# A hybrid decoder step: the 32x32 inverses of the delta net on one compact tile, and the last feed-forward block in halves of 320 and 256 tokens

## The chip, the cores and the metric

The kernel runs on one core of one Trainium2 chip. The metric is the device time of one execution in microseconds (us): the median of several timed runs. One further execution is recorded by the hardware profiler, and all traces here are of such an execution. A core has TensorE (PE, matmuls; its weight loads are a row of their own, PEld), VectorE (DVE), ScalarE (ACT), GpSimd (POOL) and SyncE (SP), which here issues the DMAs.

## The reference

Two decoder layers are computed in fp32 for 512 prompt tokens and 8 x 8 sample tokens, 576 in all, with a model width of 1024. Layer 0 mixes by trailing means (pooling), layer 1 by a gated delta rule over 16 value heads in chunks; each mixer is followed by a feed-forward network (SwiGLU, inner width 2816). Norms stand before and after each.

```
x = x + rms_norm(m, norm_mix_post[i])
h = rms_norm(x, norm_ffn_pre[i])
x = x + rms_norm(swiglu(h, ffn_w_in[i], ffn_w_out[i]), norm_ffn_post[i])
```

The delta rule needs, for each chunk and head, the solution of a unit lower triangular system:

```
t_mat = a_mat + jnp.eye(CHUNK, dtype=jnp.float32)
u = solve(t_mat, v * beta[..., None])
w = solve(t_mat, kb * jnp.exp(gc)[..., None])
```

The outputs are the 576 rows of y and the new states.

## The kernel before, in words

**Tiling.** Activations lie with channels on the partitions and tokens along the free axis. Every fp32 matrix is split into a high and a low part; `mm3` (line 979) makes one product from three matmuls for each tile of 128 channels. Weights come in tiles by a DMA (`wraw`), ACT makes the high part (`wh`) and DVE or POOL the low one (`wl`). Tokens are worked on in two ranges: `HALVES` (256 and 320) where prompt and sample are told apart, and `EVEN` (288 and 288, line 31) in the output part of the feed-forward.

**Order.** Nothing is issued as it is written. Class `Plan` records every operation with an estimated cost, makes a list schedule over the five engines, and refines it (`refined`, line 533; `moved`, line 552) by shifts of the priorities that are drawn from the seeds in the table `CHOSEN` (line 79); each string of the table is one pass over the whole program. `EITHER` operations go to DVE or POOL, as the plan finds room. Where the plan leaves TensorE idle, it inserts matmuls of a constant into a bank that is free (`ps_w`, line 527); they compute nothing that is used.

**PSUM.** `bank(tag)` (line 904) hands out the eight banks in rings: A is banks 0 to 2, B is 3 to 5, n0 and n1 are 6 and 7, and the mixer has rings of its own over the same banks (`m`, for the projections, is banks 3 and 4).

**Delta net.** The 16 heads are worked on in four groups. In `core` (line 1903) each group builds a tile `Uw` of 128 partitions by 16 systems (four heads, four spans of 128 tokens) by 128 columns. `inv32` (line 1407) inverts the four 32x32 blocks on the diagonal of all 16 systems at once. Four DVE transposes, one for each block of 32 partitions, read the block out of `Uw` with a stride of 128 elements and write it, each element twice, to `A` (in the trace `ia`); 31 steps of two DVE operations each work on `X` (in the trace `ii`); four DVE transposes put the result back into `Uw`. The blocks of 64 and 128 are then made from these by matmuls. `inv32` is woven with the sample tokens' work, and the planner lays projections of the next group beside it.

**Last feed-forward.** `ffn` (line 1148) computes the inner channels in blocks of 5, 5, 5 and 7 tiles, and adds each block's output product into `y`. In the last block (from line 1219) the two halves follow one another: for each of eight output tiles `m`, `out` (line 1173) makes the product of half 0 in ring A or of half 1 in ring B, DVE adds it to `y` (in the trace `yo`), ACT squares it (`nsq`), the squares are summed (`nacc`), and `turn_y` (line 2165) scales it (`nh`) and transposes it on TensorE, in pieces of at most 128 tokens (`PIECES`, line 34: three pieces a half), so that tokens lie on the partitions. Half 0 is transposed into ring B, half 1 into ring A. After four tiles ACT copies the transposed pieces to SBUF (`yT`); the last four stay in PSUM. `finish1` (line 2182) then sums the squares over the channels (TensorE into `ps_n`), takes square root (ACT) and reciprocal (DVE) into `nrc`, and for each piece DVE multiplies and adds the residual (`xa`, `xb`), reading `yT` and the PSUM banks; SP sends the rows out. The residual is transposed beforehand by `turn_x` (line 2146), before the gate part of this feed-forward, written to DRAM (`x_t`) and fetched again by `back_x` (line 2157).

Of the kernel before, what the change touches and what calls it, by code (L numbers as in the profile page):

```python
# [11 lines left out]
F32 = mybir.dt.float32  # L12
# [8 lines left out]
P = 128  # L21
D = 1024
# [11 lines left out]
PIECES = (((0, 128), (128, 128), (256, 32)), ((288, 128), (416, 96), (512, 64)))  # L34
# [22 lines left out]
class Plan:  # L57
# [755 lines left out]
def hybrid_kernel(  # L813
# [334 lines left out]
    def ffn(layer, x, y, wts, xp, ap_, tp, head, finish, beside=None, turn=None):  # L1148
# [24 lines left out]
        def out(bi, f0, m, hf, w):  # L1173
            s = state[hf.i]
            at = slice(hf.o, hf.o + hf.n)
            ps = bank("AB"[hf.i])[:, :hf.n]
            mm3(ps, w, lambda k: tuple(v[:, at] for v in acts[f0 + k]), blocks[bi])
            yc = y[:, m, at]
            if bi == 0:
# [1055 lines left out]
```

## Time and profile before

| | |
|---|---|
| three timed runs, median (lowest to highest) | 1526.5 us (1526.38 to 1527.4) |
| the profiled execution | 1525.06 us |
| its span, first to last instruction | 1523.3 us |
| mean granted TensorE clock | 0.997 |
| HBM read, written | 165.60 MB, 30.52 MB |

A line of a group gives operation, tile written <- tiles read, shapes and count, then busy us, mean ns of one, and the idle time of the engine before it with what ended it. A line of the table of stages gives a stretch in us from the start of the span, its length, the busy time (and instructions) of each engine, the granted TensorE clock, the DMA engines' busy share and GB/s. A line of the timeline gives start, duration, engine, line and operation; equal neighbours are merged. Operations all carry the line of the planner that issues them (L531), so tiles tell them apart.

### The profile page before, as it was taken

Reading aid. Unit: us, or ns where it says so; the run is one execution under the profiler, and the core shown is the slowest. Engines: PE = TensorE matmul, PEld = TensorE weight load, DVE = VectorE, ACT = ScalarE, POOL = GpSimd, SP = SyncE. Lnnn points to the kernel's source line nnn. Section 1 sums busy time; section 2 is a strip of 40 time slices with the busy share of each in tenths; the row PEclk is TensorE's granted clock in tenths of the full one; section 3 lists DMA queues with packets and bytes.
Section 4 is the critical chain, followed back from the end, with each engine's and each line's share of the span. In section 5 each row is a group of like instructions: output and inputs, shape, how many; then the busy total and the mean of one; then the engine's idle time right before and its main releaser. Section 6 shows DMA issues by size and latency. Waiting matters only on the chain.

```text
span 1523.3 us, 30379 instructions
## 1 busy us (share of the span) xinstructions
PE 1501.0 (99%) x11850; PEld 1452.8 (95%) x11850; DVE 1155.7 (76%) x2284; ACT 840.6 (55%) x1815; POOL 129.4 (8%) x269
## 2 busy tenths in 40 slices
PE   8999999999999999999999999999999999999997
PEld 7999999999999899899899899999999999999997
DVE  6993566678688698997899799667896476766865
ACT  7753543435466975764763764545565453534553
POOL 4210000000011010121120120100110000000000
PEclk9999999999999999999999999999999999999999
DMA  6563323233457433335433544657765333233263
GB/s 190 156 188 110 98 74 111 67 99 104 148 170 204 114 88 111 102 103 147 111 112 93 147 127 128 202 158 220 240 184 155 109 87 96 83 89 110 66 196 99
DMA packets 344902, 197.86 MB, mean 130 GB/s; under 512 B 13547, under 2 KB 337740, under 8 KB 344751
## 3 DMA queue, kind: packets, MB, share of 16 engines
q1 hardware_dynamic: 344759, 195.92, 44.6%
q8 instruction: 93, 1.52, 0.4%
q14 instruction: 50, 0.41, 0.1%
HBM read 165.60 MB, written 30.52 MB: 129 GB/s over the span
## 4 chain that ended last, share of the span: by engine, by line
PE 88%; DVE 6%; ACT 3%; DMA 2%; issue 1%; POOL 0%; SPq 0%; DVEq 0%; ACTq 0%; POOLq 0%
PE ps_B L531 29%; PE ps_A L531 26%; PE ps_m L531 19%; PE ps_s L531 5%; PE ps_k L531 5%; PE ps_x L531 2%; PE ps_e L531 1%; DVE wl L531 1%; PE ps_n L531 1%; DVE Uw L531 1%; DMA vt<-z_d 1%; DVE ac L531 1%; ACT wh L531 1%; DMA wraw<-in_gdn_w_in_dram 0%; DMA yo<-y_d 0%
## 5 line engine op out<-in xcount | busy, mean ns | idle before, releaser
L531 ACT ACTIVATE wh<-wraw 128x1024 fp32r<-128x1024 f32 (+4 forms) x239 | 232.5, 978 | 201.5 <-PE ps_B L531 79.6
L531 DVE TENSOR_TENSOR wl<-wraw,wh 128x1024 fp32r<-128x1024 f32 (+4 forms) x231 | 258.3, 1122 | 76.0 <-ACT wh L531 40.3
L531 PE MATMUL ps_m<-hH,wh 128*128 128x320 f32 (+1 forms) x832 | 251.5, 313 | 0.0
L531 PE MATMUL ps_m<-hL,wh 128*128 128x320 f32 (+1 forms) x832 | 247.5, 306 | 0.1
L531 PE MATMUL ps_m<-hH,wl 128*128 128x256 f32 (+1 forms) x832 | 245.8, 308 | 0.1
L531 PEld LDWEIGHTS ps_m<-hH,wh 128*128 128x128 f32 x832 | 155.1, 190 | 4.0 <-issue 1.0
L531 PEld LDWEIGHTS ps_m<-hL,wh 128*128 128x128 f32 x832 | 156.0, 190 | 2.0 <-issue 0.8
L531 PEld LDWEIGHTS ps_m<-hH,wl 128*128 128x128 f32 x832 | 154.7, 190 | 1.7 <-issue 0.4
L531 PE MATMUL ps_B<-hH,wh 128*128 128x320 f32 (+1 forms) x444 | 127.8, 304 | 0.2
L531 PE MATMUL ps_B<-hL,wh 128*128 128x320 f32 (+1 forms) x444 | 127.1, 304 | 0.0
L531 PE MATMUL ps_B<-hH,wl 128*128 128x320 f32 (+1 forms) x444 | 127.1, 304 | 0.0
L531 PE MATMUL ps_A<-hH,wh 128*128 128x256 f32 (+1 forms) x432 | 119.4, 292 | 0.0
L531 PE MATMUL ps_A<-hL,wh 128*128 128x256 f32 (+1 forms) x432 | 117.7, 290 | 0.0
L531 PE MATMUL ps_A<-hH,wl 128*128 128x256 f32 (+1 forms) x432 | 117.5, 291 | 0.1
L531 PE MATMUL ps_B<-aL,wh 128*128 128x288 f32 x352 | 100.0, 296 | 0.0
L531 PE MATMUL ps_B<-aH,wl 128*128 128x288 f32 x352 | 99.2, 297 | 0.7 <-DVE wl L531 0.7
L531 PE MATMUL ps_B<-aH,wh 128*128 128x288 f32 x352 | 99.1, 298 | 0.5 <-DVE xa L531 0.5
L531 PE MATMUL ps_A<-aL,wh 128*128 128x288 f32 x352 | 98.3, 296 | 0.0
L531 PE MATMUL ps_A<-aH,wl 128*128 128x288 f32 x352 | 97.7, 297 | 0.0
L531 PE MATMUL ps_A<-aH,wh 128*128 128x288 f32 x352 | 97.1, 297 | 0.0
L531 PEld LDWEIGHTS ps_B<-hH,wh 128*128 128x128 f32 x444 | 81.7, 188 | 0.7 <-ACT wh L531 0.6
L531 DVE SCALAR_TENSOR_TENSOR ac<-u,cwt,ac 128x600 f32<-128x600 f32 x96 | 79.5, 837 | 3.3 <-ACT ac L531 3.1
(463 smaller groups left out, 4040.8 us busy)
## 6 DMA issues: line engine op xcount, KB each, us to landing
wraw<-in_ffn_w_in_dram SPq DMA_DIRECT2D x77, 512.0 KB
wraw<-in_gdn_w_in_dram SPq DMA_DIRECT2D x56, 512.0 KB
graw<-in_ffn_w_in_dram SPq DMA_DIRECT2D x33, 512.0 KB
wraw<-in_ffn_w_out_dram SPq DMA_DIRECT2D x32, 448.0 KB
wraw<-in_gdn_w_out_dram SPq DMA_DIRECT2D x24, 512.0 KB
wraw<-in_ffn_w_out_dram SPq DMA_DIRECT2D x32, 320.0 KB
St<-in_state_gdn_rec_dram SPq DMA_DIRECT2D x32, 256.0 KB
out_dram<-St SPq DMA_DIRECT2D x32, 256.0 KB
```

The source lines that it names most:

```text
L531: calls[e](*a, **k)
```

## The change

In the delta net, `inv32` first copies the four diagonal blocks with ACT into one compact tile of 128 partitions by 32 by 16 (the second half of `XT`, which is free then). One DVE transpose over all 128 partitions makes `A` from it; at the end one DVE transpose over all partitions writes `X` to the compact tile, and four ACT copies put the blocks back into `Uw`.

In the last block of the last feed-forward the halves are 320 and 256 tokens (`LAST`). Both halves' products go to ring A, both halves' transposes to ring B. The pieces are 128, 128, 64 and 128, 128; the last piece holds the last 64 prompt and all 64 sample tokens and is sent out by two DMAs. In a half without a short piece, the square root and reciprocal of that piece fall away. The residual is transposed in the same five pieces. The seeds of the planner's table are others: four passes with 2281 seeds in place of six with 3239.

```diff
-PIECES = (((0, 128), (128, 128), (256, 32)), ((288, 128), (416, 96), (512, 64)))
+LAST = (Half(0, 0, 320), Half(1, 320, 256))
+PIECES = (((0, 128), (128, 128), (256, 64)), ((320, 128), (448, 128)))
...
         def out(bi, f0, m, hf, w):
...
-            ps = bank("AB"[hf.i])[:, :hf.n]
+            ends = turn is not None and bi == len(blocks) - 1
+            ps = bank("A" if ends else "AB"[hf.i])[:, :hf.n]
...
-                for hf in EVEN:
+                for hf in EVEN if turn is None else LAST:
...
+        D32 = XT[:, 1].rearrange("p (i h) -> p i h", h=16)
         for b in range(4):
             s = slice(32 * b, 32 * b + 32)
-            DVE.transpose(A[s], W[s, :, 32 * b:32 * b + 32].rearrange("p h i -> p i h").unsqueeze(2)
-                          .to_broadcast([32, 32, 2, 16]))
-            yield 1.2
+            ACT.activation(D32[s], W[s, :, s].rearrange("p h i -> p i h"), AF.Copy)
+        DVE.transpose(A, D32.unsqueeze(2).to_broadcast([P, 32, 2, 16]))
+        yield 1.2
...
+        DVE.transpose(XT[:, 1].rearrange("p (i j) -> p i j", j=32), X.rearrange("p j i -> p i j"))
         for b in range(4):
             s = slice(32 * b, 32 * b + 32)
-            DVE.transpose(W[s, :, 32 * b:32 * b + 32].rearrange("p h (i d) -> p i d h", d=2),
-                          X[s].rearrange("p j i -> p i j"))
+            ACT.activation(W[s, :, s].rearrange("p h i -> p i h"), D32[s], AF.Copy)
             yield 0.6
...
         def turn_y(hf, c):
...
-                    yT[o, c // 4] = bank("BA"[hf.i], (P, 4, P))[:n].rearrange("p c f -> p (c f)")
+                    yT[o, c // 4] = bank("B", (P, 4, P))[:n].rearrange("p c f -> p (c f)")
...
         def finish1(hf, acc):
...
-            for r, q in ((slice(0, P), slice(0, 2)), (slice(0, last), slice(2, 3))):
-                ACT.activation(rc[r, q], ps[r, q], AF.Sqrt, bias=eps_c[r], scale=1.0 / D)
-                DVE.reciprocal(rc[r, q], rc[r, q])
+            for r, q in ((slice(0, P), slice(0, whole)), (slice(0, hf.n % P), slice(whole, whole + 1))):
+                if r.stop:
+                    ACT.activation(rc[r, q], ps[r, q], AF.Sqrt, bias=eps_c[r], scale=1.0 / D)
+                    DVE.reciprocal(rc[r, q], rc[r, q])
...
-                SP.dma_start(y_prompt[0, o:o + n] if o < SEQ else y_sample.rearrange("b t d -> (b t) d"), xT[o])
+                m = min(n, SEQ - o)
+                SP.dma_start(y_prompt[0, o:o + m], xT[o][:m])
+                if m < n:
+                    SP.dma_start(y_sample.rearrange("b t d -> (b t) d"), xT[o][m:])
```

More of the change, by code (lines that the diff above doesn't have):

```diff
@@ L2148, in turn_x @@
                 for c4 in range(0, NC, 4):
-                    ps = bank("n%d" % (o >= EV), (P, 4, P))[:n]
+                    ps = bank("n%d" % (o >= LAST[1].o), (P, 4, P))[:n]
                     for c in range(4):
@@ L2159, in back_x @@
             xa = xp.tile([P, 4, D], F32, name="xa", tag="x", bufs=1)
-            xb = ap_.tile([P, 2, D], F32, name="xb1", tag="tb", bufs=1)
+            xb = ap_.tile([P, D], F32, name="xb1", tag="tb", bufs=1)
             for i, (o, n) in enumerate(PIECES[0] + PIECES[1]):
-                xT[o] = (xa[:n, i] if i < 4 else xb[:n, i - 4])
+                xT[o] = xa[:n, i] if i < 4 else xb[:n]
                 SP.dma_start(xT[o], x_t[o:o + n])
@@ L2170, in turn_y @@
             if c == 3:
-                sbs = [ap_.tile([P, k, 4 * P], F32, name="yT", tag="graw", bufs=2) for k in (2, 1)]
+                sbs = [ap_.tile([P, 2, 4 * P], F32, name="yT", tag="graw", bufs=2) for _ in PIECES[hf.i][::2]]
             for i, (o, n) in enumerate(PIECES[hf.i]):
                 if c % 4 == 0:
-                    yT[o, c // 4] = bank("BA"[hf.i], (P, 4, P))[:n].rearrange("p c f -> p (c f)")
+                    yT[o, c // 4] = bank("B", (P, 4, P))[:n].rearrange("p c f -> p (c f)")
                 ps = yT[o, c // 4]
@@ L2186, in finish1 @@
             rc = halftile(tp, "nrc", hf, 1, (P, 4))
-            last = PIECES[hf.i][2][1]
+            whole = hf.n // P
             for i, (o, n) in enumerate(PIECES[hf.i]):
-                n = n if i == 2 else P
-                a = acc[0]
-                PE.matmul(ps[:n, i:i + 1], a[:, i * P:i * P + n] if i < 2 else a[:, EV - n:], ones[:, 0:1],
-                          start=True, stop=True)
-            for r, q in ((slice(0, P), slice(0, 2)), (slice(0, last), slice(2, 3))):
-                ACT.activation(rc[r, q], ps[r, q], AF.Sqrt, bias=eps_c[r], scale=1.0 / D)
-                DVE.reciprocal(rc[r, q], rc[r, q])
+                PE.matmul(ps[:n, i:i + 1], acc[0][:, o - hf.o:o - hf.o + n], ones[:, 0:1], start=True, stop=True)
+            for r, q in ((slice(0, P), slice(0, whole)), (slice(0, hf.n % P), slice(whole, whole + 1))):
+                if r.stop:
+                    ACT.activation(rc[r, q], ps[r, q], AF.Sqrt, bias=eps_c[r], scale=1.0 / D)
+                    DVE.reciprocal(rc[r, q], rc[r, q])
             for i, (o, n) in enumerate(PIECES[hf.i]):
```

341 rows, old and new, of the table CHOSEN are left out of this document.

## The prediction

> **What bounds the kernel now.** I read the page's first part, then a table of stages, then the timeline where the table shows a hole.
>
> ```profile
> span 1523.3 us, 30379 instructions
> PE 1501.0 (99%) x11850; PEld 1452.8 (95%) x11850; DVE 1155.7 (76%) x2284; ACT 840.6 (55%) x1815; POOL 129.4 (8%) x269
> ```
>
> TensorE is busy 1501.0 of 1523.3 us, so work taken from another engine is worth only what TensorE waits for that engine. The profiled execution took 1525.06 us, 1.8 more than its span; the median of the three timed runs is 1526.5. Differences are worked out in the trace and put on the median.
>
> ```profile
> core 0: us, PE busy (x) PEld busy (x) DVE busy (x) ACT busy (x) POOL busy (x), PEclk, DMA share, GB/s
> 487.00:1047.00 560.00, 554.71 (x4749) 516.28 (x4748) 469.01 (x1100) 353.91 (x1000) 78.39 (x154) 1.00 0.45 128
> 560.00:925.00 365.00, 361.01 (x3138) 335.45 (x3137) 324.73 (x777) 227.35 (x681) 58.29 (x122) 1.00 0.40 114
> 1180.00:1440.00 260.00, 260.00 (x1959) 259.74 (x1958) 177.41 (x272) 114.49 (x175) 0.00 (x0) 1.00 0.32 92
> 1458.00:1481.00 23.00, 23.00 (x177) 22.77 (x176) 14.79 (x25) 13.46 (x22) 0.00 (x0) 1.00 0.72 208
> 1489.00:1513.00 24.00, 23.82 (x182) 23.52 (x181) 12.59 (x23) 10.43 (x19) 0.00 (x0) 1.00 0.27 88
> ```
>
> The rows are the delta net, its busiest part, most of the last feed-forward, and the first and second half of its last output block. Two things are to be seen. In the delta net VectorE is busy 324.73 of 365 us (89%), yet TensorE sits idle only 560.00 - 554.71 = 5.3 us of the whole stage. And between the halves of the last block, from 1481 to 1489, lies a hole. Its timeline:
>
> ```profile
> 1481.23 0.29 PE L531 MATMUL ps_A<-aH,wl 128*128 128x288 f32 x1
> ...
> 1484.46 1.28 PE L527 MATMUL ps_w<-ones 128*128 128x128 f32 x10
> ...
> 1487.60 1.41 DVE L531 SCALAR_TENSOR_TENSOR xa<-ps_B,nrc,xa 128x512 f32<-128x512 f32 x2
> ...
> 1488.40 0.40 PE L531 MATMUL ps_B<-aH,wh 128*128 128x288 f32 x1 [0.47 <-DVE xa L531]
> ```
>
> The first half's last product issues at 1481.23, in a bank of ring A. The second half's first product, in ring B, starts at 1488.40, when VectorE's final multiply-add has read ps_B. That is the mechanism: the first half's transposed output stays in ring B until its norm is known, and the second half's products are given the same three banks. TensorE meanwhile issues "ps_w" matmuls, which only fill time: the busy share hides the wait.
>
> **The last block's rings.** What TensorE does between 1481.4 and 1488.3, grouped:
>
> ```profile
> L531 PE MATMUL ps_B<-ident,nh 128*128 128x128 f32 x9 | 2.4, 307 | 1.3 <-ACT nh L531 0.8 <-DVE nacc L531 0.3 <-ACT yT L531 0.2
> L527 PE MATMUL ps_w<-ones 128*128 128x128 f32 x16 | 2.3, 276 | 0.0
> L531 PE MATMUL ps_B<-ident,nh 128*32 128x128 f32 x5 | 1.4, 275 | 0.1
> L531 PE MATMUL ps_n<-ones,nacc 128*128 128x1 f32 x4 | 0.5, 232 | 0.0
> L531 PE MATMUL ps_n<-ones,nacc 128*32 128x1 f32 x2 | 0.2, 181 | 0.0
> ```
>
> Needed are 9 + 5 transposes and 6 small sums, 20 instructions. Back to back such a matmul costs 0.11 us: ten fillers take 1.28 us, the last 0.28 long, (1.28 - 0.28)/9. So 2.2 us is work, and the rest of 1488.40 - 1481.23 - 0.13 = 7.04 us is waiting: 4.8 us. After the change both halves multiply into ring A, whose banks are emptied by short adds, and both transpose into ring B. The second half can start at once; its own transposes are the ones that now wait for the norm, but they come one product later and sit beside products. The needed 2.2 us stays. **Gain 4.8 us.** What hides the norm then is 20 us of products. If VectorE is late there, PE has three ring-A banks, over 7 us, before it feels it; what is late next is the second half's first transposes, which need the same multiply-adds done.
>
> **The split 320 and 256.** Rates come from stretches of one width, 256 and then 320:
>
> ```profile
> 60.00:77.00 17.00, 17.00 (x144) 17.00 (x144) 16.63 (x32) 12.02 (x23) 4.86 (x4) 1.00 0.61 175
> 90.00:130.00 40.00, 40.00 (x273) 39.77 (x273) 28.14 (x35) 20.07 (x28) 0.00 (x0) 1.00 0.52 149
> ```
>
> 17.00/144 = 118.1 ns and 40.00/273 = 146.5 ns; 288 columns cost 260.00/1959 = 132.7. The block has 7 x 3 x 8 = 168 matmuls a half: 168 x (146.5 + 118.1) = 44.45 us against 336 x 132.7 = 44.59. **Zero.**
>
> Pieces of at most 128 tokens fall from six to five. The residual x and the output y are transposed piece by piece, eight channel tiles each: 8 transposes go from x, 8 from y. Those of x stand in a full TensorE stream before the last feed-forward: 8 x 0.11 = **0.9 us**; the two ACT copies and DMAs that go with them are off the path. Those of y are all of the second half, and at least ten of its 24 run after its last product (rows below), where nothing waits for TensorE: I count 3 x 0.11 = **0.3 us**.
>
> **The tail.**
>
> ```profile
> 1514.47 0.66 PE L531 MATMUL ps_A<-ident,nh 128*128 128x128 f32 x4
> 1515.09 0.73 DVE L531 SCALAR_TENSOR_TENSOR xa<-yT,nrc,xa 128x512 f32<-128x512 f32 x1
> 1515.46 0.95 PE L531 MATMUL ps_A<-ident,nh 128*64 128x128 f32 x6 [0.33 <-ACT nh L531]
> ...
> 1517.83 1.80 SPq L531 DMA_DIRECT2D out_dram<-xb  x2
> 1518.38 0.73 DVE L531 SCALAR_TENSOR_TENSOR xb<-ps_A,nrc,xb 64x512 f32<-64x512 f32 x1
> ```
>
> Six multiply-adds run one behind another from 1515.09 to 1519.11, 0.66 us apart, whatever their partitions (128 or 64, 0.73 us each); then the last output DMA is issued, and its landing ends the span at 1523.3. With two pieces of 128 there are four: -2 x 0.66 = -1.32. One square root and reciprocal pair on a short piece goes too, about 0.1. Against it, the last piece holds 64 prompt and 64 sample rows and needs two DMAs, both behind the last multiply-add, where before one was. On SP two neighbouring issues stand 0.4 apart:
>
> ```profile
> 1454.66 1.29 SPq L531 DMA_DIRECT2D xa<-x_t  x3
> ```
>
> (1.29/3 = 0.43). Bytes and landing stay about alike. **Gain 1.3 + 0.1 - 0.4 = 1.0 us**; bounds 0.2 (the two DMAs in turn cost twice that) and 1.8 (they overlap, and the earlier first piece counts).
>
> **The 32x32 inverses.** Per group of four heads' chunks (four groups):
>
> ```profile
> L531 DVE STREAM_TRANSPOSE ia<-Uw 32x1024 f32<-32x1024 f32 x16 | 32.6, 2034 | 0.2
> L531 DVE STREAM_TRANSPOSE Uw<-ii 32x512 f32<-32x512 f32 x16 | 18.2, 1138 | 0.4
> L531 DVE STREAM_TRANSPOSE T<-Uw 32x512 f32<-32x512 f32 x12 | 8.4, 701 | 0.3
> L531 ACT ACTIVATE qk<-ac 128x512 f32<-128x512 f32 x16 | 10.0, 629 | 0.6 <-DVE ac L531 0.5
> ```
>
> Gone are 4 x 2.03 + 4 x 1.14 = 12.7 us of VectorE. Added are one transpose of 128x1024 from a dense tile and one of 128x512 back, and 4 + 4 ACT copies of 32x512. No row shows a 128-partition transpose. Lower end: the dense rate of T<-Uw, 2 x 0.70 = 1.4, plus 1.14; upper end: four blocks in turn, as before. I take the lower, 2.5 us, since the multiply-adds above cost the same on 128 and on 64 partitions. So VectorE loses 10 us a group, 40 of the stage's 469. A copy at the ACT row's rate is 0.63 us: 5 us of ACT a group, 20 in all, on 353.91 of 560. The copies read or write W with a stride; the nearest row for that is VectorE's, strided 1138 against dense 701, so the upper end is 629 x 1138/701 = 1.02 us a copy, 33 in all. The chain of one inverse goes from 12.7 us to 2.5 + 5.0 = 7.5 (10.7 at the upper end), which matters little, as TensorE has other groups' products beside it. Queued behind each row of four copies on ACT is the emptying of PSUM.
>
> The Trainium skill ("SBUF — State Buffer", Door 1: The DMA port swizzle) says that SBUF accesses run at full rate only while they stay within 16-byte lines, four fp32. By it the strided copies sit at the upper end, 13 us more of ACT; the transposes' two rows agree in kind, no row of ACT shows it, and the sum below holds under either, as long as ACT has the slack.
>
> What is it worth? What TensorE waits for in the stage, by its waits and its fillers:
>
> ```profile
> PE ps_x L531 <- DVE vt L531: 2.4, 3, 1.0
> PE ps_x L531 <- DVE rn L531: 0.5, 1, 0.5
> L527 PE MATMUL ps_w<-ones 128*128 128x128 f32 x36 | 5.7, 278 | 0.0
> L531 PE MATMUL ps_m<-hH,wh 128*128 128x320 f32 x448 | 144.6, 325 | 0.0
> L531 PE MATMUL ps_B<-hH,wh 128*128 128x320 f32 x240 | 68.5, 312 | 0.2
> ```
>
> Idle 5.3 plus fillers 36 x 0.11 = 4.0 gives 9.3 us at most; 2.9 of it is put down to VectorE by name. I take **2 us**. Bounds: 9.3, and a loss, because the program's planner orders every instruction anew, with other numbers in its table. How much order is worth here shows in the last two rows: the same 320-column matmul lasts 13 ns longer amid this stage than in the feed-forward; 13 ns over 3 x 448 such matmuls is 17 us. I let a better or worse order move a third of that, 5 us.
>
> **Sum:** 4.8 + 0.9 + 0.3 + 1.0 + 2 = 9.0 us. 1526.5 - 9.0 = 1517.5 us (the profiled execution: 1516.1).
>
> **Rivals.**
> - *VectorE's relief opens the delta net.* All 9.3 us of waits go: 1526.5 - 7.0 - 9.3 = 1510.2. For it: 89% VectorE. Against: only 2.9 us name VectorE. The weight loads give a wider view: 335.45 busy of 365 here, 259.74 of 260 in the feed-forward, so 29 us lack. The Trainium skill ("Trainium Kernel Development and Optimization", Performance Expectations) holds weight-load share, not matmul share, for the measure of headroom; by it more than 9.3 us may be to be had.
> - *The new order costs.* The 5 us loss in place of the 2 us gain: 1526.5 - 7.0 + 5 = 1524.5, and anything between. For it: every stage is reordered; against: the feed-forward, where TensorE is 100% busy, hardly feels order.
> - *The second half starves.* It starts at once and finds no weights: it had 7 us to fetch three tiles ahead. For it: 448 KB each 2.5 us (21 x 118.1 ns) is 180 GB/s. Against: the first half ran with TensorE 23.00 of 23.00 busy at 208 GB/s. Price: all of the 4.8: 1522.3.
> - *ACT becomes the wait* (slower). A projection product is 24 x 146.5 ns = 3.5 us, and its ring has two banks; four copies in a row keep ACT from emptying one for 2.5 us at 0.63, 4.1 at 1.02. Beyond 3.5 us TensorE stands still, eight times. The kernel is slower by over 0.2% when eight stretches expose more than 7.0 + 3.1 us, 1.3 each, that is from 1.2 us a copy (4 x 1.2 = 4.8 = 3.5 + 1.3). At 1.3 us a copy: 8 x 1.7 = 14, 1526.5 - 7.0 + 14 = 1533. Against: ACT is 63% busy, and the planner can spread the copies.
> - *It does not do what it says*: 128-partition transposes cost four blocks in turn. Then VectorE gains nothing, and 1526.5 - 7.0 = 1519.5, inside the forecast.
>
> **How the numbers follow.** Forecast, 1513 to 1520.5 (VectorE's share from nothing to 6): 56 in 100. Opened delta net, 1508 to 1513: 12. Costly order, 1520.5 to 1525: 16. Starved half, 1521 to 1524: 5. ACT, over 1529.6: 11. 0.2% is 3.05 us, about what a measurement can tell: under 1523.45 is faster, 56 + 12 + 9 + 4 = 81; within, 7 + 1 = 8; slower 11. Range 1510 to 1524.5: it leaves out the ACT case and the ends of two others.
>
> **What would show it.** No row where the second half's first product waits for VectorE's xa, and 16 fewer fillers: right on the rings. Second-half products named ps_A, 118 ns apart; four multiply-adds at the end, and two DMAs behind the last. Transposes of 128 partitions near 1.4 and 1.14 us, ACT copies near 0.63. Wrong if the delta net's TensorE waits name ACT, if the stage (560 us now) grows by over 5, or if the hole comes back as waits for weights.

## The result and the profile after

The changed kernel takes 1528.1 us (median of 12 runs, 1525.5 to 1536.5), the kernel before 1526.8 (12 runs, 1525.0 to 1529.2): a ratio of 1.0014, with a 95% interval of 1.0005 to 1.0023. That is no gain, and at most a loss of 0.23%, where 1517.5 was forecast. The profiled execution took 1526.48 us, against 1525.06 before.

The first part of the page of the changed kernel:

```profile
span 1524.8 us, 30248 instructions
PE 1493.7 (98%) x11782; PEld 1447.1 (95%) x11782; DVE 1126.6 (74%) x2277; ACT 871.8 (57%) x1842; POOL 107.6 (7%) x249
```

VectorE is relieved by 29 us, ACT has 31 more, and TensorE's busy time falls by 7.3 us while the span grows by 1.5: it waits more. To see where, I cut the span at four instructions of TensorE. The first and the last product of the delta net's projections and the first and the last of the output block are, in the timeline of the changed kernel:

```profile
482.34 0.31 PE L471 MATMUL ps_m<-hH,wh 128*128 128x320 f32 x1
...
1053.74 0.31 PE L471 MATMUL ps_m<-hH,wl 128*128 128x320 f32 x1
...
1464.68 0.31 PE L471 MATMUL ps_A<-aH,wh 128*128 128x320 f32 x1
...
1512.26 0.28 PE L471 MATMUL ps_A<-aH,wl 128*128 128x256 f32 x1
```

and in that of the kernel before:

```profile
481.50 0.31 PE L531 MATMUL ps_m<-hH,wh 128*128 128x320 f32 x1
...
1045.75 0.31 PE L531 MATMUL ps_m<-hH,wl 128*128 128x320 f32 x1
...
1457.77 0.29 PE L531 MATMUL ps_A<-aH,wh 128*128 128x288 f32 x1
...
1511.79 0.29 PE L531 MATMUL ps_B<-aH,wl 128*128 128x288 f32 x1
```

| stage, us | before | after | difference | predicted |
|---|---|---|---|---|
| up to the first projection | 481.50 | 482.34 | +0.8 | 0 |
| delta net | 564.25 | 571.40 | **+7.15** | -2 |
| from there to the last output block | 412.02 | 410.94 | -1.1 | -0.9 |
| last output block | 54.02 | 47.58 | **-6.4** | -5.1 |
| its last product to the end | 11.52 | 12.52 | **+1.0** | -1.0 |
| span | 1523.31 | 1524.78 | +1.5 | -9.0 |

So the output block gives what was forecast and a little more; the delta net takes it back. The table of stages of the changed kernel, columns as in the prediction:

```profile
487.00:1047.00 560.00, 542.79 (x4661) 506.29 (x4660) 435.69 (x1083) 381.04 (x1014) 58.86 (x138) 1.00 0.44 126
560.00:925.00 365.00, 353.65 (x3084) 329.71 (x3084) 301.63 (x771) 256.38 (x700) 47.59 (x111) 1.00 0.40 113
1464.00:1490.00 26.00, 26.00 (x184) 25.94 (x183) 15.07 (x23) 13.92 (x22) 0.00 (x0) 1.00 0.64 182
1490.00:1513.00 23.00, 23.00 (x193) 22.79 (x192) 15.95 (x32) 13.43 (x26) 0.00 (x0) 1.00 0.42 127
```

In the first row VectorE is busy 435.69 us where it was 469.01, ACT 381.04 where it was 353.91, and TensorE now idles 560.00 - 542.79 = 17.2 us where it idled 5.3. Fillers fell from 36 to 4, so waits and fillers together went from 9.3 us to 17.2 + 4 x 0.11 = 17.6: +8.3, a little more than the whole loss of the stage. The last two rows are the output block, with no hole left.

Who is waited for, in the waits of TensorE in this stage:

```profile
PE ps_m L471 <- ACT u L471: 5.1, 4, 1.7
PE ps_k L471 <- DVE QD L471: 2.0, 3, 1.1
PE ps_x L471 <- DVE vt L471: 1.7, 2, 1.1
PE ps_k L471 <- DMA St<-in_state_gdn_rec_dram: 1.7, 1, 1.7
PE ps_k L471 <- ACT Uw L471: 1.7, 3, 0.8
PE ps_x L471 <- ACT ac L471: 1.2, 1, 1.2
PE ps_k L471 <- ACT sn L471: 1.1, 1, 1.1
PE ps_x L471 <- DMA crow<-in_state_gdn_conv_dram: 1.0, 1, 1.0
PE ps_m L471 <- ACT zz L471: 0.8, 2, 0.5
PE ps_x L471 <- ACT nco L471: 0.5, 1, 0.5
```

A row gives who waits, for whom, the us in total, how often, and the longest. The rows that name ACT add up to 10.4 us; in the kernel before it was one, of 0.2. The largest row is new: projections (ps_m) wait until ACT has emptied their ring into u. What ACT did then, in its timeline, with the waiting product behind it:

```profile
654.90 4.51 ACT L471 ACTIVATE ii<-Uw 32x512 f32<-32x512 f32 x4
659.43 0.50 ACT L471 ACTIVATE u<-ps_m 128x256 f32<-128x256 f32 x2
```

```profile
659.98 0.41 PE L471 MATMUL ps_m<-hH,wh 128*128 128x320 f32 x1 [1.56 <-ACT u L471]
```

Four of the new copies in a row take 4.51 us, not 2.5; the emptying of PSUM stands behind them, and TensorE stands still for 1.56 us. Grouped by form, the new operations are:

```profile
L471 ACT ACTIVATE ii<-Uw 32x512 f32<-32x512 f32 x16 | 17.9, 1120 | 1.7 <-DVE Uw L471 1.6
L471 ACT ACTIVATE Uw<-ii 32x512 f32<-32x512 f32 x16 | 17.8, 1112 | 1.9 <-DVE ii L471 1.7
L471 DVE STREAM_TRANSPOSE ia<-ii 128x1024 f32<-128x1024 f32 x4 | 5.0, 1245 | 6.9 <-ACT ii L471 6.9
L471 DVE STREAM_TRANSPOSE ii<-ii 128x512 f32<-128x512 f32 x4 | 4.3, 1080 | 0.1
```

The transposes over 128 partitions take 1245 and 1080 ns, 2.3 us together: the lower end of the prediction. The copies take 1.12 us, 35.7 in all, above its upper end of 1.02.

### The profile page after: what moved, and what is told of

Same layout as the page of the kernel before. It is cut to its first block, busy times and chain, and to the rows that moved or that the text cites. A ratio compares the mean times of both kernels' runs of the same rounds, so it can differ in the third digit from the quotient of the medians.

```text
span 1524.8 us, 30248 instructions
## 1 busy us (share of the span) xinstructions
PE 1493.7 (98%) x11782; PEld 1447.1 (95%) x11782; DVE 1126.6 (74%) x2277; ACT 871.8 (57%) x1842; POOL 107.6 (7%) x249
## 4 chain that ended last, share of the span: by engine, by line
PE 83%; DVE 7%; ACT 5%; DMA 3%; issue 2%; POOL 0%; SPq 0%; ACTq 0%; DVEq 0%; POOLq 0%
PE ps_B L471 27%; PE ps_A L471 27%; PE ps_m L471 16%; PE ps_s L471 5%; PE ps_k L471 4%; PE ps_x L471 2%; DVE wl L471 1%; ACT Uw L471 1%; ACT ii L471 1%; PE ps_n L471 1%; ACT wh L471 1%; DVE ii L471 1%; PE ps_e L471 1%; DVE Uw L471 1%; DVE nacc L471 1%
## 5 line engine op out<-in xcount | busy, mean ns | idle before, releaser
L471 DVE TENSOR_TENSOR wl<-wraw,wh 128x1024 fp32r<-128x1024 f32 (+4 forms) x238 | 266.9, 1124 | 89.1 <-ACT wh L471 55.3
L471 PE MATMUL ps_m<-hH,wl 128*128 128x320 f32 (+1 forms) x832 | 244.6, 308 | 0.0
L471 PE MATMUL ps_A<-aH,wl 128*128 128x288 f32 (+2 forms) x408 | 111.7, 296 | 0.0
L471 PE MATMUL ps_A<-aL,wh 128*128 128x288 f32 (+2 forms) x408 | 111.2, 296 | 0.0
L471 PE MATMUL ps_A<-aH,wh 128*128 128x288 f32 (+2 forms) x408 | 111.1, 296 | 0.0
L471 PE MATMUL ps_B<-aH,wh 128*128 128x288 f32 x296 | 84.0, 297 | 0.0
L471 PE MATMUL ps_B<-aH,wl 128*128 128x288 f32 x296 | 83.5, 296 | 0.1
L471 PE MATMUL ps_B<-aL,wh 128*128 128x288 f32 x296 | 83.1, 295 | 0.0
L471 PEld LDWEIGHTS ps_B<-hH,wl 128*128 128x128 f32 x444 | 81.9, 188 | 0.7 <-DVE wl L471 0.4
```

The source lines that it names most:

```text
L471: calls[e](*a, **k)
```

## The experiments

**What is to be told apart.** The theory: the length of the copies makes the delta net's new waits. Its rival: the new order makes them, with four strings of seeds in place of six, and would with any copies. The tail and what each half of the change is worth alone are separate questions; e1 added one more, a loss in the head of the kernel.

One difficulty stands ahead of all. The planner's table of seeds fits one program with one set of estimated costs; an edit that changes any cost reorders everything. So e1, e5, e6 and e10 keep the changed kernel's order exactly: the edited operations keep the planner's price. e2, e3, e7, e8, e9, e11, e12 and e13 have their order written out as a table, spliced from the plans of the two kernels or, in e7 and e11, the changed kernel's with the last block rearranged:

```diff
-        for chosen in self.CHOSEN:
-            best = self.refined(best, chosen)
...
+        raw.frombytes(zlib.decompress(base64.b85decode(self.ORDER)))
...
+            for d, k, e in zip(raw[:n], raw[n:2 * n], raw[2 * n:]):
```

**e1_dense_copies**: the changed kernel in its own order, with the compact tile laid out so that the copies read and write runs of 32 elements; the stride goes to the two transposes.

```diff
-        D32 = XT[:, 1].rearrange("p (i h) -> p i h", h=16)
+        D32 = XT[:, 1].rearrange("p (h i) -> p h i", h=16)
...
-            ACT.activation(D32[s], W[s, :, s].rearrange("p h i -> p i h"), AF.Copy)
-        DVE.transpose(A, D32.unsqueeze(2).to_broadcast([P, 32, 2, 16]))
+            ACT.activation(D32[s], W[s, :, s], AF.Copy)
+        DVE.transpose(A, D32.rearrange("p h i -> p i h").unsqueeze(2).to_broadcast([P, 32, 2, 16]))
...
-        DVE.transpose(XT[:, 1].rearrange("p (i j) -> p i j", j=32), X.rearrange("p j i -> p i j"))
+        DVE.transpose(D32.rearrange("p h (i d) -> p i d h", d=2), X.rearrange("p j i -> p i j"))
...
-            ACT.activation(W[s, :, s].rearrange("p h i -> p i h"), D32[s], AF.Copy)
+            ACT.activation(W[s, :, s], D32[s], AF.Copy)
```

> Copies theory: the changed kernel's delta net is longer because each ACT copy of a 32x32 block row takes 1.12 us with its stride where the plan priced 0.63, so that ACT is late for TensorE. With dense copies in the very same order of instructions they take about 0.63 us, the one transpose that now reads with a stride takes 2.0 instead of 1.25, and the delta net gives back most of its 7 us: about 1522 us. Order theory: the new order itself is worse; the same order with shorter copies stays within 2 us of the changed kernel's 1528.

Measured: 1516.9 us against 1526.0, a ratio of 0.9952 (0.9934 to 0.9970). The executions fall into two groups, 1513.6 to 1517.5 and 1522.6 to 1526.8; the profile is one of the second, and what sets them apart lies ahead of the delta net (last section). The groups of the copies and transposes in e1:

```profile
L471 ACT ACTIVATE Uw<-ii 32x512 f32<-32x512 f32 x16 | 10.1, 628 | 2.2 <-DVE ii L471 1.9
L471 ACT ACTIVATE ii<-Uw 32x512 f32<-32x512 f32 x16 | 10.0, 627 | 1.9 <-DVE Uw L471 1.7
L471 DVE STREAM_TRANSPOSE ia<-ii 128x1024 f32<-128x1024 f32 x4 | 8.3, 2078 | 0.8 <-ACT ii L471 0.7
L471 DVE STREAM_TRANSPOSE ii<-ii 128x512 f32<-128x512 f32 x4 | 4.6, 1161 | 0.1
```

The stride's cost has moved: 15.6 us off ACT, 3.6 us onto VectorE, since there it is paid by 8 instructions in place of 32. The waits of the stage in e1, the largest two:

```profile
PE ps_x L471 <- DVE vt L471: 2.7, 4, 1.0
PE ps_k L471 <- DMA St<-in_state_gdn_rec_dram: 2.2, 2, 2.0
```

No projection waits for u any more. Its delta net runs from

```profile
492.66 0.31 PE L471 MATMUL ps_m<-hH,wh 128*128 128x320 f32 x1
...
1053.30 0.31 PE L471 MATMUL ps_m<-hH,wl 128*128 128x320 f32 x1
```

560.64 us, 10.8 less than the changed kernel's 571.40, in the same order of instructions, and more than the 7 that the change had lost. (e10 below has the same order and the same copies there, and its delta net takes 557.59: two profiles of the same stage can differ by 3 us, so the gain is 11 to 14.) Waits that name ACT are 0.4 us in e1 where they were 10.4. The theory of the copies holds: the order alone cannot have made these waits.

**e5_in_dense** and **e6_out_dense**: only one side dense, in the same order; e5 the copies out of `Uw`, e6 those back into it.

```diff
+        DD = XT[:, 1].rearrange("p (h i) -> p h i", h=16)
...
-            ACT.activation(D32[s], W[s, :, s].rearrange("p h i -> p i h"), AF.Copy)
-        DVE.transpose(A, D32.unsqueeze(2).to_broadcast([P, 32, 2, 16]))
+            ACT.activation(DD[s], W[s, :, s], AF.Copy)
+        DVE.transpose(A, DD.rearrange("p h i -> p i h").unsqueeze(2).to_broadcast([P, 32, 2, 16]))
```

```diff
-        DVE.transpose(XT[:, 1].rearrange("p (i j) -> p i j", j=32), X.rearrange("p j i -> p i j"))
+        DVE.transpose(DD.rearrange("p h (i d) -> p i d h", d=2), X.rearrange("p j i -> p i j"))
...
-            ACT.activation(W[s, :, s].rearrange("p h i -> p i h"), D32[s], AF.Copy)
+            ACT.activation(W[s, :, s], DD[s], AF.Copy)
```

> The changed kernel's order, with dense copies only into the compact tile; the copies back into the working tile stay strided (1.12 us). If both places hold ACT alike, half of the 11 us that dense copies gave: about 1522 us; if only the way in matters, 1517; if only the way back, 1528.

> The mirror image: strided copies in, dense copies back. Alike: 1522 us; if only the way back matters (the combination to 64 and 128 waits for it), 1517; if only the way in, 1528.

Measured: e5 1523.95 us, 0.9989 (0.9973 to 1.0005); e6 1522.1, 0.9977 (0.9960 to 0.9994). The delta net lasts 567.5 us in e5 and 566.2 in e6, 3.9 and 5.2 less than 571.4, together 9.1 of the 10.8. Each place costs a good part of the loss, so it is not one bad spot in the chain; that they cost alike isn't shown, since 1.3 us between them is less than the 3 by which e1 and e10 differ.

**e4_four_passes**: the kernel before, with the first four of its six strings of seeds, so nothing but order.

```diff
     CHOSEN = (
...
-        "0: 34167 89976 38559 26485 54844 54754 3144 34359 29600 15343 66724 89421; 1: 11879 98376 83436 48878 "
...
```

> The kernel before with the first four of its six passes of seeds alone, so that only the order changes. Order theory (fewer passes leave a worse order): 4 to 8 us longer in the delta net, over 1530. Copies theory: within 2 us of 1526.5.

Measured: 1534.45 us, 1.0056 (1.0044 to 1.0068); the delta net takes 569.8 us in place of 564.25. So what the rival builds on is real as well: order alone, with every operation as before, moves this kernel by 8 us. It isn't what the new waits of the changed kernel are made of, but a change that comes with another table of seeds carries a term of this size, of unknown sign.

**e2_rings_only** and **e3_inverses_only**: each half of the change alone, the order of the two plans spliced where the delta net ends. e2 has the inverses of before, e3 the last block of before (both shown against the changed kernel):

```diff
-            ACT.activation(D32[s], W[s, :, s].rearrange("p h i -> p i h"), AF.Copy)
-        DVE.transpose(A, D32.unsqueeze(2).to_broadcast([P, 32, 2, 16]))
+            DVE.transpose(A[s], W[s, :, 32 * b:32 * b + 32].rearrange("p h i -> p i h").unsqueeze(2)
+                          .to_broadcast([32, 32, 2, 16]))
...
```

```diff
-            ps = bank("A" if ends else "AB"[hf.i])[:, :hf.n]
+            ps = bank("AB"[hf.i])[:, :hf.n]
...
-                for hf in EVEN if turn is None else LAST:
+                for hf in EVEN:
...
```

> The last block's part alone (320 and 256, rings by use, five pieces), with the inverses of before and the order of before up to the end of the delta net, the changed kernel's order behind it. Both theories: the last block is 6.4 us shorter and the tail 1 us longer, as in the changed kernel's trace, so 1520 to 1522 us. Rival, that the block's gain depends on what the delta net leaves late: 1526.

> The inverses' part alone, with the changed kernel's order up to the end of the delta net and the order of before behind it. Both theories: 7 us longer than before, 1533 to 1535 us; if the delta net's loss came from something that the last block changed, 1527.

Measured: e2 1523.7 us, 0.9983 (0.9974 to 0.9992); e3 1537.0, 1.0070 (1.0052 to 1.0087). The signs are as in the table of stages: e2's last block takes 47.5 us, e3's delta net 572.7. Both lose some 3 us where the orders meet: from the delta net to the last block e2 takes 414.0 us and e3 415.2, where the kernel before takes 412.0 and the changed kernel 410.9.

**e12_rings_good_seam** and **e13_inverses_seam**: the same two, with the place where the orders meet chosen anew; nothing else is edited.

> The last block's part alone, as in the earlier such run, with the order of before up to 1044 us and the changed order behind it; the seam is put where no prefetch is broken. Last block 6.4 us shorter, tail 1 us longer, the residual's transposes 0.9 us less: 1519.5 to 1521 us. If the earlier run's 1523.7 was not the seam, 1523 again.

> The inverses' part alone (strided copies, the changed order) up to the end of the delta net, the order of before behind it, with a better seam. Delta net 571 instead of 564 us, and the head of the change: 1533 to 1535 us. With the part above, the two should add up to about the changed kernel's 1528.

Measured: e12 1521.3 us, 0.9968 (0.9956 to 0.9980); e13 1540.1, 1.0083 (1.0060 to 1.0106). e12 is 5.3 us faster than the kernel before, with its last block at 47.5 us and its delta net at 564.6. So the block does alone what it does in the changed kernel, 6.5 us less. The whole of this half was forecast at 7.0 us: the tail is 1.0 us longer instead of shorter, and from the delta net to the last block it still takes 413.9 us, 3 more than in the changed kernel. e13's executions again lie in two groups, 1533.4 to 1538.0 and 1542.2 to 1544.9, the profile in the second; its delta net takes 570.2 us, 6 more than before. So the inverses' half alone is slower by about 8 us in the first group, of three executions. -5.3 + 8 = 2.7 is near the whole change's +1.3, and the rest is of the size of what is lost where orders meet; with all six executions, the median of which is 13.5 slower, the sum does not come out.

**e11_rings_undone**: e1 with the rings as before, but 320/256 kept, in e1's order as far as the old rings allow it.

```diff
-            ps = bank("A" if ends else "AB"[hf.i])[:, :hf.n]
+            ps = bank("AB"[hf.i])[:, :hf.n]
...
-                    yT[o, c // 4] = bank("B", (P, 4, P))[:n].rearrange("p c f -> p (c f)")
+                    yT[o, c // 4] = bank("BA"[hf.i], (P, 4, P))[:n].rearrange("p c f -> p (c f)")
```

> Dense copies, halves of 320 and 256 and five pieces as in the change, but the rings as before: half 0 multiplies in A and transposes into B, half 1 the other way round. The order is the changed kernel's, except where that would lock. If the shared ring makes the hole between the halves, 4.8 us come back there and the time is about 1522; if the split does it, nothing changes from 1517.

Measured: 1540.3 us, 1.0094 (1.0079 to 1.0108). Its last block takes 69.0 us, 21 more than with the rings divided. In the worst stretch TensorE is busy half the time and the granted clock is 0.76:

```profile
1480.00:1490.00 10.00, 5.23 (x27) 4.48 (x26) 4.49 (x9) 5.38 (x11) 0.00 (x0) 0.76 0.49 137
```

The direction is right, the size says little: the kernel before had an order made for its rings, and its hole was 7 us. The nearest to what the rings are worth is e12's last block, 6.5 us, which has the split and the pieces in it; no run has the rings alone.

**e7_early_finish**: on the tail; e1 with half 0's sums, root and multiply-adds issued early, not amid the last products.

> Dense copies, and in the last block the first half's last transposes, sums, norm, six multiply-adds and DMAs are issued as soon as their inputs are there, instead of amid the second half's last products; the rest of the order is kept. If the changed kernel's longer tail (12.5 us from the last product to the end, before 11.5) comes from these crowding VectorE, the tail falls to 11.3 us or less and the time by 1 to 1.5 us against the dense copies alone, to about 1515.5. If it comes from the two DMAs behind the last multiply-add, the tail stays at 12.5.

Measured: 1518.7 us, 0.9952 (0.9940 to 0.9965). From last product to end it takes 11.97 us instead of 12.5, so half of what had been lost comes back; but the last block takes 50.8 us where the changed kernel takes 47.6. The stretch of its second half:

```profile
1474.00:1507.00 33.00, 30.75 (x244) 29.72 (x243) 22.74 (x40) 19.64 (x36) 0.00 (x0) 1.00 0.41 125
```

TensorE is busy 30.75 of 33 us. Its named waits in this block are 1.0 us for an add that empties ring A (yo) and 0.7 for the low parts of weights (wl), both VectorE's, and the changed kernel's block has none: put early, the multiply-adds delay other work of VectorE that TensorE needs. The planner's late place for them was the better one.

**e10_act_queue**: e1 with the last output DMA, that of the sample rows, issued from ACT's queue, so that the two last DMAs start together.

```diff
+    SPA = plan.engine(SP=nc.scalar)
...
-                    SP.dma_start(y_sample.rearrange("b t d -> (b t) d"), xT[o][m:])
+                    SPA.dma_start(y_sample.rearrange("b t d -> (b t) d"), xT[o][m:])
```

> Dense copies in the changed kernel's order, and the very last output DMA (the 64 sample rows) issued from ACT instead of SP, so that the two DMAs behind the last multiply-add go out side by side. If the second issue in turn costs the tail 0.4 to 0.8 us, the time from the last product to the end falls from 12.5 to 11.9 us; if the landing of the two transfers ends the span anyway, it stays at 12.5. The total moves by less than the scatter of the runs.

Measured: 1517.5 us, 0.9954 (0.9941 to 0.9968), as e1. Both DMAs are issued at once, on SP and on ACT:

```profile
1517.27 0.48 SPq L471 DMA_DIRECT2D out_dram<-xb  x1
```

```profile
1517.27 0.55 ACTq L471 DMA_DIRECT2D out_dram<-xb  x1
```

and the span ends at 1522.2, 5.0 us later; issued one after the other in the changed kernel, it ended 4.9 us after the first. The second issue was not on the path.

**e8_head_of_before** and **e9_head_seam**: e1 with the order of the kernel before up to 245 us (e8) or about 240 us (e9, where the two orders meet better), and the change's order behind. Only the table of the order differs from e1.

> Dense copies, with the order of before up to 245 us (the middle of the first feed-forward) and the changed order behind it. If the head's order is what makes some executions 10 us longer at a lower granted clock (with dense copies 4 of 12 lay at 1522 to 1527, the others at 1513.5 to 1517.5; before has none), all runs lie within 3 us of each other near 1515; if it is chance, a third stays high.

> As the run with the head of before, but with the seam 10 us earlier, where it breaks no weight prefetch (the other seam left TensorE idle for 6 us between 240 and 300 us). Head theory (the order of the first 50 us decides whether the clock falls back a second time): no execution 10 us above the rest, all within 4 us, median 1513 to 1516, which is below both kernels. Chance: a quarter of the executions at 1522 or more.

Measured: e8 1520.6 us, 0.9969 (0.9956 to 0.9981); e9 **1513.4 us, 0.9917 (0.9905 to 0.9930)**, the fastest version, better than both kernels by 13 and 15 us. Where the orders meet, e8 idles 6 us, and e9 does not:

```profile
240.00:300.00 60.00, 53.83 (x390) 53.19 (x389) 37.29 (x58) 22.69 (x32) 0.00 (x0) 0.94 0.29 85
```

```profile
230.00:290.00 60.00, 60.00 (x456) 60.00 (x455) 41.16 (x64) 24.62 (x35) 0.00 (x0) 1.00 0.30 88
```

In e9 the delta net takes 559.05 us, 5.2 less than before, the last block 47.5, 6.5 less, and the tail 12.5, 1.0 more. No execution of either fell into a later group (e8 1520.0 to 1523.6, e9 1512.8 to 1514.6).

## Why the prediction was wrong, point by point

- **The rings: right.** "Gain 4.8 us", and 0.3 of transposes; the whole block fell by 6.4. The second half's first product no longer waits; it starts amid the first half's last:

```profile
1488.01 0.43 PE L471 MATMUL ps_A<-aH,wh 128*128 128x256 f32 x2
```

  From the block's first product to its last TensorE is busy 47.58 of 47.58 us, with no filler where there were 16. The 1.3 us above 5.1 are nearly all transposes: 20 of y's run inside the block where 33 did, 13 fewer and not the three that were counted, 10 x 0.11 = 1.1 us more. Five of them have only moved behind the last product, 20 there in place of 15.
- **The split: right.** The products' 44.45 us and 20 transposes and 6 small sums at 0.11 make 47.3 of the block's 47.58 us, so 320 and 256 columns cost what was reckoned. The eight transposes of the residual that fall away agree with the 1.1 us seen before the block (0.9 predicted), which no run isolated.
- **The 128-partition transposes: right, at the lower end** (2.3 us for the two, 2.5 taken). VectorE lost 33 us in the stage where 40 were taken: the transposes themselves went from 32.6 + 18.2 to 5.0 + 4.3 us, 41.5 less, but GpSimd has 20 us less there (58.86 for 78.39), and VectorE is only 7 instructions short in all (2277 for 2284) with 24 transposes gone: it has taken over operations that were GpSimd's.
- **The price of a copy: wrong, and this is the step that failed.** "A copy at the ACT row's rate is 0.63 us", with 1.02 as the upper end. It was 1.12. The row that I took was dense; the ratio for the upper end, 1.62, was that of another engine. The Trainium skill ("SBUF — State Buffer", Door 1: The DMA port swizzle) was named there for the upper end, its rule being that consecutive accesses run at full bandwidth while they hit the same 16-byte line, and that each step to a new line costs. The rows agree in kind: 627 ns dense and 1120 with a stride of 512 bytes, 1.8 times.
- **"The sum below holds under either as long as ACT has the slack": wrong.** ACT has slack as a mean (68% busy in the stage's row) and none at the eight places where four copies stand in a row. The prediction's own price for those, 4 copies less 3.5 us, gives 8 x (4.48 - 3.5) = 7.8 us at 1.12; measured were 10.8 in the same order. The rival "ACT becomes the wait" was the mechanism, and its formula gives 1526.5 - 7.0 + 7.8 = 1527.3 us, where 1528.1 was measured. That it comes so near is in part luck: the trace has not eight waits for u but four, of 5.1 us, and 5.3 more that name ACT elsewhere. At the upper end of 1.02 it would already have cost 8 x 0.58 = 4.6 us, which the sum and the range should have carried; it got 11 in 100 and only the price of a copy above 1.2.
- **"the planner can spread the copies": wrong.** It can only avoid what it foresees, and its estimate for ACT doesn't look at the stride. This line of its costs makes a copy of 512 elements 0.833 x 512 + 205 = 632 ns:

```
t = 0.833 * max(n, 16) + (170 if ps else 205) + extra
```

  That fits e1's 627 ns and not the kernel's 1120. The plan laid products beside copies that took nearly twice their time; fillers, which it puts where it foresees TensorE idle, fell to 4. How much of the 10.8 us a plan with the true price would save was not tried.
- **VectorE's relief: right in sign, too small.** With dense copies the delta net takes 557.6 to 561.2 us in the six runs that have them (e1, e7 to e11), 3.1 to 6.7 less than before, where 2 were taken. The bounds held it. What part of it is order stays open: e4 shows order moving the same stage by 5.6. That e1's 1516.9 us is nearly the forecast's 1517.5 is luck in part: this term and the block came out better than forecast, the tail by 2 us worse.
- **The opened delta net** did not come; of its 9.3 us, 3.1 to 6.7 came with dense copies. The Trainium skill ("Trainium Kernel Development and Optimization", Performance Expectations) was named for a wider headroom by weight-load share: after the change that share is 329.71 of 365, no higher than the 335.45 before, so no run here shows those 29 us to be had.
- **The tail: wrong sign.** Four multiply-adds in place of six saved time, as predicted. What was left out is that half 0's are now late: its norm does hide behind the "20 us of products", but its multiply-adds reach past the last of them. VectorE after the last product (1512.26):

```profile
1512.58 0.42 DVE L471 TENSOR_TENSOR yo<-yo,ps_A 128x256 f32<-128x256 f32 x1
1512.91 0.74 DVE L471 SCALAR_TENSOR_TENSOR xa<-ps_B,nrc,xa 128x512 f32<-128x512 f32 x1
1513.58 0.41 DVE L471 TENSOR_TENSOR nacc<-nacc,nsq 128x256 f32<-128x256 f32 x1
1513.91 0.74 DVE L471 SCALAR_TENSOR_TENSOR xa<-ps_B,nrc,xa 64x512 f32<-64x512 f32 x1
1514.57 0.41 DVE L471 TENSOR_TENSOR nacc<-nacc,nsq 128x256 f32<-128x256 f32 x1
1516.35 0.17 DVE L471 RECIPROCAL nrc<-nrc 128x2 f32<-128x2 f32 x1 [1.38 <-ACT nrc L471]
...
1519.08 0.74 DVE L471 SCALAR_TENSOR_TENSOR xb<-ps_B,nrc,xb 128x512 f32<-128x512 f32 x1
```

  The last sum of squares starts 2.31 us after the last product; before, it started 1.36 after it:

```profile
1513.15 0.46 DVE L531 TENSOR_TENSOR nacc<-nacc,nsq 128x288 f32<-128x288 f32 x1 [0.57 <-ACT nsq L531]
```

  Two multiply-adds of half 0 stand in front of it: that is the +1.0. In e7, which has them early, the sum starts 1.28 us after the last product, but only half of the 1.0 reaches the end. From the reciprocal on the two kernels take alike (8.43 and 8.44 us): the multiply-adds end 0.77 us earlier against the reciprocal, and the last DMAs take 0.76 longer to end the span. "Bytes and landing stay about alike" was wrong there. e10 rules out the second issue. The DMA rows suggest bytes, which no run tests: the changed kernel issues the last 1024 KB (512, 256 and 256) within 1.2 us, from 1519.20 to 1520.38, the kernel before its last 1152 KB (512, 384 and 256) within 2.0, from 1517.17 to 1519.14.
- **Order.** "A third of that, 5 us" was a fair size: e4 shows 5.6 in this stage and 8 in all.

## What to carry to other kernels

Price an operation that reads or writes with a stride from a row of the same engine with that stride, and if there is none, carry the full cost of the upper end through every queue behind it, not through the engine's mean load. Where a stride must be paid, put it on the operation that is issued least often: here 8 transposes instead of 32 copies turned a loss of 1 us into a gain of 9, and of 13 with the better head. A planner with a wrong price for an operation can't keep clear of the wait that it makes, and the parts of a change to a planned kernel can only be compared in the same order of instructions.

## What the runs showed of the hardware that was not expected

**A second fall of the clock.** The two groups of e1 and e13 differ by about 10 us that are lost between 35 and 56 us from the start. Their table of stages for 34 to 57 us, first the kernel before, then e1:

```profile
34.00:57.00 23.00, 22.94 (x172) 21.62 (x172) 20.83 (x57) 17.73 (x48) 5.11 (x7) 1.00 0.37 111
```

```profile
34.00:57.00 23.00, 23.00 (x103) 21.44 (x102) 11.93 (x32) 11.06 (x28) 2.84 (x4) 0.55 0.15 48
```

TensorE is all but fully busy in both, yet the granted clock is 0.55 in e1, and 103 matmuls are done where 172 were. It is a second fall because the first 34 us have one too, with 0.90 in the kernel before and 0.85 in e1. The profiles of e5, e10 and e13 show the second one as well, all the others do not. With the head in the changed kernel's order it comes in some executions and not in others (4 of e1's 12 lie in the later group, none of e7's 5); with the head of the kernel before (e2, e8, e9, e12) the runs show no such group. What in that head decides it is open.

**A stretch at half clock in the delta net.** Inside the changed kernel's delta net there is a stretch of 3.41 us at half clock. The 8 us ahead of it, and the stretch:

```profile
700.00:708.15 8.15, 6.52 (x100) 5.61 (x98) 3.71 (x6) 6.28 (x9) 1.47 (x2) 1.00 0.23 58
708.15:711.56 3.41, 3.41 (x63) 3.29 (x60) 0.30 (x2) 1.20 (x5) 0.00 (x0) 0.50 0.98 282
```

The profiles of e3, e4, e5, e6 and e13 have one such stretch in their delta nets too, of 3.41 or 6.83 us at 0.50; those of the kernel before, of e2 and e12, and of all versions with dense copies on both sides have none. In each case TensorE had been busy for only 75 to 88% of the 8 to 10 us ahead of it. If the waits bring it on, they cost a second time: an estimate for the changed kernel is half of 3.41, 1.7 us of the 10.8. It doesn't follow every such wait, though: e1's TensorE is busy for 8.20 of the 10 us from 969, and its clock stays at 1.00. What decides it is open, and no run isolates it.

**The landing of the last rows.** Two output DMAs issued in the same moment from two queues (e10) ended no sooner than two issued in turn: 5.0 us from issue to the end of the span against 4.9.
